# Shared weight places, ordered scores, squares summed on TensorE, and search state in PSUM, in a two-layer hybrid trunk

## The chip, the cores and the metric

The kernel runs on one core of one Trainium2 chip. The metric is device microseconds of one execution. The rows below come from one profiled execution of the kernel before.

## What is computed

The reference runs two residual layers over 1024 tokens of width 1024, and a final RMSNorm. Each layer is `h = h + mixer(rmsnorm(h))`, then `h = h + mlp(rmsnorm(h))`.

```python
# layer 0's mixer: sparse attention beside a pooling mixer
rel   = relu(einsum('bqhd,bsd->bqhs', qi, ki))
score = einsum('bqhs,bqh->bqs', rel, wi) * IDX_DIM ** -0.5     # causal
_, idx = lax.top_k(score, 256)                                 # per query
prob  = softmax(q @ k[idx] * Dh ** -0.5);  ya = prob @ v[idx]
yb    = (trailing means over 2/4/8/16 tokens - token) @ pool_w * pool_scale
out   = concat([ya, yb]) @ w_out
# layer 1's mixer: gated DeltaNet (short convolution, chunked delta rule)
# each MLP, hidden 4096
out   = square(relu(h @ w1)) @ w2
def rmsnorm(x, g): return x * rsqrt(mean(x * x, -1) + 1e-6) * g
```

## The kernel before

The tokens are kept transposed, in two halves of 512: `h[0]` and `h[1]`, each eight tiles of 128 features by 512 tokens. A full-precision product is three TensorE matmuls of 512 columns (`mm3`, L241 to L243) over values split in a high and a low part. Weights come in chunks of 256 KB: a DMA into a "raw" tile, a ScalarE copy that makes the high part (L167), and a GpSimd subtraction that makes the low part (L171). `prefetch` (L192) does this for a stream ("a", "m", or the layer 1 output weights "o"), into the rings that `room` gave the stream. A chunk takes two tiles of its ring, so ring "w" (4 tiles) has two places; the ring "wo" (2 tiles) has one, and stream "o" is loaded with `ahead=0`, which is when its chunk is wanted.

`norm_scale` squares the eight tiles on ScalarE (L301), adds them on VectorE (`add_square`, L304), sums the 128 partitions with four matmuls against a column of ones (`rstd_cols`, L284), takes the reciprocal root in twelve small VectorE operations (L260 to L265), and spreads the result over partitions with four transposes (L272).

`topk` (L607) finds each query's threshold bit by bit: 31 steps, each building a candidate (L655), counting scores against it (L629 on VectorE, L657 on ScalarE for some blocks), comparing the counts (L669) and keeping the candidate where it held (L670). Queries of blocks 2 and 3 are searched together in a stretch at 94 to 198 us, blocks 4 to 7 in another at 456 to 620 us. All small state of the search lies in SBUF. The steps run as a background job: the code that issues matmuls calls `tick`.

A scheduler orders each engine's instructions by the order in which the code names them and by priority. In the second stretch the first half's MLP is laid beside the search: `beside(us)` issues about that many microseconds of its matmuls between steps, with the amounts in `BESIDE` (L105): for index scores, for kept projections and the search, for the second attention, and for what remains of the background once the search is done. `next(att)` yields one step of attention. `odd_heads` does the same for layer 1, and takes the norm of `h[1]` before layer 1 at about 1654 us and of `h[0]` at about 947 us. `finish` (L1346) does the final norm of a half and writes it out.

PSUM has eight banks of 512 columns. In layer 0 they are 2 for "g", 1 for "o" and 5 for "t".

Of the kernel before, what the change touches and what calls it, by code (L numbers as in the profile page):

```python
# [35 lines left out]
BANKS = {"even": {"g": 2, "o": 1, "t": 5}, "odd": {"g": 2, "o": 1, "d": 2, "t": 3}}  # L36


C_ID, C_ONE = 0, P
C_ALL = P + 2  # L40
# [20 lines left out]
def const_tables():  # L61
# [4 lines left out]
    c[:, C_ONE:C_ONE + 2] = 1.0  # L66
# [38 lines left out]
BESIDE = (4.0, 3.4, 2.2, 6.0)  # L105


class Ring:


    def __init__(self, pool, name, n, cols, usual=None):
        self.pool, self.name, self.n, self.cols, self.usual = pool, name, n, cols, usual or cols
        self.count = 0
# [12 lines left out]
class Trunk:  # L126
    def __init__(self, ctx, tc, I, out):
# [8 lines left out]
        self.ident, self.ones = self.ca[:, C_ID:C_ID + P], self.ca[:, C_ONE:C_ONE + 2]  # L136
        wp = self.pool("weights")
        self.W, self.WM, self.raw = Ring(wp, "w", 4, 512), Ring(wp, "wm", 4, 512), Ring(wp, "raw", 4, 512)
# [40 lines left out]
    def plan(self, **streams):  # L179
# [3 lines left out]
        self.rings, self.ahead, self.loaded = {}, {}, dict.fromkeys(streams, 0)  # L183
# [95 lines left out]
    def rstd_cols(self, sq, n, out=None):  # L279

        nc = self.nc
        ps = self.bank()
        for c in range(4):
            nc.tensor.matmul(ps[:, 2 * c:2 * c + 2], sq[:, c * P:(c + 1) * P], self.ones[:, 0:2], start=True, stop=True)  # L284
# [5 lines left out]
    def norm_scale(self, h):  # L290
        return self.rstd(self.squares(h), D)
# [15 lines left out]
    def norm(self, h, gain, ring=None):  # L307

        return self.normed(h, gain, self.norm_scale(h), ring)
# [53 lines left out]
    def gained(self, h, k, x):  # L363

        nc = self.nc
        f, gain = self.T.get(), self.prm[:, R_MIX + k:R_MIX + k + 1]
# [6 lines left out]
    def even_scales(self, acc):  # L373

        r = self.rstd_cols(acc, D, self.small(4, "even_r"))
# [6 lines left out]
    def even_first(self):  # L382
# [9 lines left out]
        acc = self.T.get()  # L392
        for k in range(KT):
# [4 lines left out]
            if k + 1 < KT:  # L398
                load(k + 1)
            if k == KT - 2:  # L400
                nc.sync.dma_start(self.ca, self.I["ca"])
                nc.sync.dma_start(self.cx, self.I["ce"])
            self.gained(h, k, x)
            sq = self.T.get() if k else acc
            nc.scalar.activation(sq, h[k], AF.Square)
            if k:
                nc.vector.tensor_tensor(acc, acc, sq, op=OP.add)
# [8 lines left out]
        self.even_scales(acc)  # L416
# [4 lines left out]
    def even_second(self):  # L421
# [7 lines left out]
        self.even_scales(self.squares(hs))  # L429
# [177 lines left out]
    def topk(self, blocks, nv):  # L607
# [12 lines left out]
        cnt, sg, cur, cand, keep, t1, t2, most, top = (  # L620
# [821 lines left out]
```

## Time and profile before

| | us |
|---|---|
| median of 3 runs | 2864.97 |
| their range | 2862.25 to 2869.15 |
| the profiled execution | 2867.0 |
| its span, first to last instruction | 2865.2 |
| TensorE busy | 2678.5 (93%) |
| VectorE busy | 1711.5 (60%) |
| GpSimd busy | 1248.2 (44%) |
| ScalarE busy | 1187.8 (41%) |
| mean granted TensorE clock | 0.969 of 2.4 GHz |

A timeline line gives the start, the duration in us, the engine, the line of code, the operation, what is written from what is read, and in brackets the idle time before it with what ended it. A line of a view by line gives, after the bar, the time in us, the mean in ns of one, and the idle time before. In the view of stretches the columns of busy time are PE (TensorE), PEld (its weight loads), DVE (VectorE), ACT (ScalarE) and POOL (GpSimd), then the granted clock, the DMA share and GB/s.

### The profile page before, as it was taken

What the parts mean: (1) busy time and instruction counts of PE and PEld (TensorE: products, weight loads), DVE (VectorE), ACT (ScalarE), POOL (GpSimd) and SP (SyncE); (2) the same over time, 40 slices, a digit from 0 to 9 for tenths busy, and PEclk for the clock granted to TensorE, in tenths of its full rate; (3) what the DMA queues carried; (4) which work ended last, traced back from release to release, by engine and by line L of the source; (5) the groups of instructions that cost most, each with busy time, mean ns of one, the idle gap of its engine ahead of it and who ended that gap; (6) DMA issues with size and microseconds to landing.
All of it is one profiled execution on the core that took longest, in us unless ns stands there. A gap on an engine that the chain in (4) does not pass through costs nothing. (4 is left out here: it accounts for less than half of the span.)

```text
span 2865.2 us, 44751 instructions
## 1 busy us (share of the span) xinstructions
PE 2678.5 (93%) x16648; PEld 2105.1 (73%) x16648; DVE 1711.5 (60%) x3653; ACT 1187.8 (41%) x2475; POOL 1248.2 (44%) x1074
## 2 busy tenths in 40 slices
PE   8788997988999899999999999899999999899997
PEld 6556775766777677887777767677777777688886
DVE  6894469997524645564655677755655644733334
ACT  4545455763433443343432444433333323333332
POOL 6642536442234544444444444444443434544442
PEclk9889999998999899999999999999999999999999
DMA  5221222220112222222222211122222222333332
GB/s 166 60 73 41 92 67 85 84 90 30 49 61 80 75 80 79 74 71 78 74 81 72 75 52 53 56 71 70 75 75 74 64 67 85 100 109 97 96 96 77
DMA packets 119917, 218.82 MB, mean 76 GB/s; under 512 B 13970, under 2 KB 15122, under 8 KB 119698
## 3 DMA queue, kind: packets, MB, share of 16 engines
q1 hardware_dynamic: 119698, 215.95, 24.3%
q8 instruction: 131, 2.15, 0.3%
q14 instruction: 88, 0.72, 0.1%
HBM read 207.51 MB, written 4.19 MB: 74 GB/s over the span
## 5 line engine op out<-in xcount | busy, mean ns | idle before, releaser
L171 POOL TENSOR_TENSOR wm<-raw,wm 128x512 fp32r<-128x512 f32 x437 | 581.1, 1330 | 904.5 <-ACT wm L167 880.7
L167 ACT ACTIVATE wm<-raw 128x512 fp32r<-128x512 f32 x437 | 274.4, 628 | 690.7 <-PE ps_g L242 344.2
L171 POOL TENSOR_TENSOR w<-raw,w 128x512 fp32r<-128x512 f32 x196 | 259.1, 1322 | 310.2 <-ACT w L167 296.4
L827 DVE TENSOR_TENSOR h<-ps_d,h 128x512 f32<-128x512 f32 x392 | 266.6, 684 | 154.2 <-PE ps_d L243 152.2
L241 PE MATMUL ps_g<-x,w 128*128 128x512 f32 x648 | 265.0, 409 | 8.8 <-ACT w L167 7.2
L242 PE MATMUL ps_g<-x,w 128*128 128x512 f32 x648 | 263.7, 407 | 6.2 <-POOL x L171 4.0
L813 DVE SCALAR_TENSOR_TENSOR ps_g<-ps_g,temps 128x512 f32<-128x512 f32 x128 | 89.1, 696 | 300.7 <-ACT temps L811 300.7
L243 PE MATMUL ps_g<-x,w 128*128 128x512 f32 x648 | 263.3, 406 | 1.8 <-POOL w L171 1.8
L241 PE MATMUL ps_d<-y,wm 128*128 128x512 f32 x596 | 247.2, 415 | 7.6 <-DVE h L827 6.3
L242 PE MATMUL ps_d<-y,wm 128*128 128x512 f32 x596 | 238.9, 401 | 0.0
L243 PE MATMUL ps_d<-y,wm 128*128 128x512 f32 x596 | 238.5, 400 | 0.2 <-POOL wm L171 0.2
L167 ACT ACTIVATE w<-raw 128x512 fp32r<-128x512 f32 x196 | 122.9, 628 | 277.1 <-PE ps_g L242 208.4
L241 PE MATMUL ps_g<-xb,wm 128*128 128x512 f32 x512 | 204.7, 400 | 11.9 <-DVE y L171 7.6
L243 PE MATMUL ps_g<-xb,wm 128*128 128x512 f32 x512 | 204.4, 399 | 4.5 <-POOL wm L171 4.4
L242 PE MATMUL ps_g<-xb,wm 128*128 128x512 f32 x512 | 204.4, 399 | 0.6 <-POOL xb L171 0.6
L934 DVE SCALAR_TENSOR_TENSOR qkvz<-temps,conv,qkvz 128x512 f32<-128x512 f32 x144 | 137.3, 953 | 110.2 <-ACT qkvz L932 109.3
L241 PE MATMUL ps_g<-x,wm 128*128 128x512 f32 (+1 forms) x396 | 158.4, 400 | 6.1 <-ACT wm L167 4.7
L243 PE MATMUL ps_g<-x,wm 128*128 128x512 f32 (+1 forms) x396 | 157.7, 398 | 0.7 <-POOL wm L171 0.7
L242 PE MATMUL ps_g<-x,wm 128*128 128x512 f32 (+1 forms) x396 | 158.1, 399 | 0.0
L241 PEld LDWEIGHTS ps_g<-x,w 128*128 128x128 f32 x648 | 126.7, 196 | 41.1 <-ACT w L167 7.6
L242 PEld LDWEIGHTS ps_g<-x,w 128*128 128x128 f32 x648 | 126.0, 195 | 36.3 <-POOL x L171 5.3
L827 DVE TENSOR_TENSOR h<-ps_t,h 128x512 f32<-128x512 f32 x184 | 125.8, 686 | 42.4 <-PE ps_t L243 41.8
(446 smaller groups left out, 6134.9 us busy)
## 6 DMA issues: line engine op xcount, KB each, us to landing
raw<-in_w_dram SPq DMA_DIRECT2D x512, 256.0 KB, 2.6
raw<-in_woi_dram SPq DMA_DIRECT2D x128, 256.0 KB, 2.6
raw<-in_wei_dram SPq DMA_DIRECT2D x52, 256.0 KB, 2.7
raw<-in_weo_dram SPq DMA_DIRECT2D x32, 256.0 KB, 2.6
raw<-in_woo_dram SPq DMA_DIRECT2D x32, 256.0 KB, 2.7
h<-in_xt_dram SPq DMA_DIRECT2D x16, 256.0 KB, 3.7
out_dram<-temps SPq DMA_DIRECT2D x16, 256.0 KB, 2.1
at<-at SPq DMA_DIRECT2D x48, 64.0 KB, 2.0
```

Of the source, the lines that this page charges most:

```text
L167: self.nc.scalar.activation(out, in_, AF.Copy)
L171: eng.tensor_tensor(lo, full, hi.bitcast(F32), op=OP.subtract)
L241: mm(ps, wh, xh, start=start, stop=False)
L242: mm(ps, wh, xl, start=False, stop=False)
L243: mm(ps, wl, xh, start=False, stop=stop)
L813: nc.vector.scalar_tensor_tensor(ps, ps, 0.0, r, op0=OP.max, op1=OP.mult)
L827: nc.vector.tensor_tensor(h, ps, h, op=OP.add)
L934: nc.vector.scalar_tensor_tensor(acc, pin[:, j:j + 512], cw(j), acc, op0=OP.mult, op1=OP.add)
```

## The change

It has five parts.

1. Places. Ring "w" has two tiles instead of four. Layer 0 gets a second ring "w2" of two tiles, and layer 1 a ring "wo" of four tiles, shared by streams "a" and "o". `prefetch` takes the ring whose next place was loaded longest ago.
2. Sums of squares. `summed_squares` sums eight square tiles on TensorE into one PSUM accumulation: four matmuls of two columns for each tile, 32 a norm instead of four and seven VectorE additions. It is used for the first projection of each half, and for the norms that go through `norm`, which now include the one of `h[1]` before layer 1, and for `finish` of the second half. The ones come from a memset.
3. Search state. In `topk`, `cur`, `keep` and `top` lie in a PSUM bank "s" of their own; `cnt`, `cand`, `sg`, `most`, `t1` and `t2` stay in SBUF. Bank "t" has four instead of five.
4. Scale by gain. `gained` computes the low part with one VectorE operation instead of a VectorE multiplication and a subtraction on VectorE or GpSimd.
5. Order. The first eight steps of the second attention are each issued behind the last matmul so far, with 3.0 us of MLP after each. `BESIDE` changes.

```diff
-BANKS = {"even": {"g": 2, "o": 1, "t": 5}, ...}
+BANKS = {"even": {"g": 2, "o": 1, "s": 1, "t": 4}, ...}
-BESIDE = (4.0, 3.4, 2.2, 6.0)
+BESIDE = (4.0, 2.6, 2.8, 9.0, 3.0)
-        self.W, ... = Ring(wp, "w", 4, 512), ...
+        self.W, ... = Ring(wp, "w", 2, 512), ...
@@ prefetch
-            ring = rings[self.loaded[st] % len(rings)]
-            self.loaded[st] += 1
+            ring = min(rings, key=lambda r: r.loads[0])
+            self.loaded += 1
+            ring.loads.append(self.loaded)
+    def add_columns(self, ps, sq, start, stop):
+        for c in range(4):
+            self.nc.tensor.matmul(ps[:, 2 * c:2 * c + 2], sq[:, c * P:(c + 1) * P], self.ones[:, 0:2],
+                                  start=start and c == 0, stop=stop and c == 3)
+    def summed_squares(self, h):
+        ps = self.bank()
+        for k, t in enumerate(h):
+            sq = self.T.get()
+            self.nc.scalar.activation(sq, t, AF.Square)
+            self.add_columns(ps, sq, k == 0, k == KT - 1)
+        return ps
@@ norm
-        return self.normed(h, gain, self.norm_scale(h), ring)
+        return self.normed(h, gain, self.norm_scale(h, True), ring)
@@ gained
-        nc.vector.tensor_scalar(f, h[k], gain, None, op0=OP.mult)
...
-        self.rest(t[:, 512:1024], f, t[:, 0:512], k % 2 == 0)
+        nc.vector.scalar_tensor_tensor(t[:, 512:1024], h[k], gain, t[:, 0:512].bitcast(F32), op0=OP.mult, op1=OP.subtract)
@@ topk
-        cnt, sg, cur, cand, keep, t1, t2, most, top = (
-            small(n) for n in ("cnt", "sg", "cur", "cand", "keep", "t1", "t2", "most", "top"))
+        cnt, sg, cand, t1, t2, most = (small(n) for n in ("cnt", "sg", "cand", "t1", "t2", "most"))
+        state = self.bank("s")
+        cur, keep, top = (state[:, n * G:(n + 1) * G] for n in range(3))
@@ odd_heads
-                x[s] = self.normed(self.h[s], R_MIX + 8, self.norm_scale(self.h[s]))
+                x[s] = self.norm(self.h[s], R_MIX + 8)
@@ even layer, rings
-            self.room("a", self.W, self.WM, self.W, self.WM, self.W)
+            self.W2 = Ring(ep, "w2", 2, 512)
+            self.room("a", self.W, self.WM, self.W2)
@@ second attention
-                with self.tc.issue_after(self.last_matmul()):
-                    next(att)
+                for _ in range(8):
+                    with self.tc.issue_after(self.last_matmul()):
+                        next(att)
+                    beside(BESIDE[4])
@@ odd layer, rings
-            self.room("a", self.W, ahead=1)
-            self.room("o", Ring(op, "wo", 2, 512), ahead=0)
+            more = Ring(op, "wo", 4, 512)
+            self.room("a", self.W, more, ahead=1)
+            self.room("o", more, ahead=0)
@@ finish
-        r = self.norm_scale(self.h[s])
+        r = self.norm_scale(self.h[s], s == 1)
```

Three places show how instructions stand. The first is VectorE's row in a search of two blocks; `tk_cur`, `tk_keep` and `tk_top` are SBUF tiles, `ps_s` the new bank. Before:

```order
L655 TENSOR_SCALAR tk_cand<-tk_cur 128x2
L629 TENSOR_SCALAR junk,tk_cnt<-mask_76,tk_cand 128x384
L557 TENSOR_TENSOR temps<-ps_g,rb 128x512
L669 TENSOR_TENSOR tk_keep<-tk_cnt,tk_top 128x2
L559 COPY uhist<-temps 128x16
L670 COPY_PREDICATED tk_cur<-tk_keep,tk_cand 128x2
```

And after:

```order
L674 TENSOR_SCALAR tk_cand<-ps_s 128x2
L648 TENSOR_SCALAR junk,tk_cnt<-mask_78,tk_cand 128x384
L688 TENSOR_TENSOR ps_s<-tk_cnt,ps_s 128x2
L689 COPY_PREDICATED ps_s<-ps_s,tk_cand 128x2
L674 TENSOR_SCALAR tk_cand<-ps_s 128x2
L648 TENSOR_SCALAR junk,tk_cnt<-mask_78,tk_cand 128x384
```

The four operations of a step keep their order; L655, L669 and L670 have become L674, L688 and L689 with an operand in PSUM, and the counting operation has none.

The second place is TensorE at the norm of `h[1]` before layer 1; L284 and L289 are the column sums, L272 and L273 the transposes. Before:

```order
L241 MATMUL ps_d<-yh,wo 128x512
L284 MATMUL ps_t<-ca,temps 128x2 x4
L242 MATMUL ps_d<-yh,wo 128x512
L243 MATMUL ps_d<-yh,wo 128x512
L241 MATMUL ps_d<-y,wo 128x512
...
L241 MATMUL ps_d<-yh,wo 128x512
L242 MATMUL ps_d<-yh,wo 128x512
L272 MATMUL ps_t<-ca,rs_y 128x128 x4
```

And after:

```order
L242 MATMUL ps_d<-y,wm 128x512
L243 MATMUL ps_d<-y,wm 128x512
L244 MATMUL ps_d<-y,wm 128x512
L289 MATMUL ps_t<-ones,temps 128x2 x32
L273 MATMUL ps_t<-ca,rs_y 128x128 x4
L1074 MATMUL ps_t<-xxc,lm 32x32 x4
L1078 MATMUL ps_t<-dy,xtc 32x32 x4
```

Before, thirteen wide matmuls stand between the sums and the transposes; now the eight sets of sums stand together and nothing stands between them and the transposes.

The third place is the end of TensorE's row, at the final norm of the second half. Before:

```order
L242 MATMUL ps_t<-y,wm 128x512
L243 MATMUL ps_t<-y,wm 128x512
L284 MATMUL ps_t<-ca,temps 128x2 x4
L272 MATMUL ps_t<-ca,rs_y 128x128 x4
L1438 UNCONDITIONAL_BRANCH
```

And after:

```order
L243 MATMUL ps_t<-y,wm 128x512
L244 MATMUL ps_t<-y,wm 128x512
L289 MATMUL ps_t<-ones,temps 128x2 x32
L273 MATMUL ps_t<-ca,rs_y 128x128 x4
L1463 UNCONDITIONAL_BRANCH
```

All eight sets stand behind the last wide matmul.

## Rows read from the trace of the kernel before

**Rows 1.** The page's first part: busy time of each engine.

```profile
PE 2678.5 (93%) x16648; PEld 2105.1 (73%) x16648; DVE 1711.5 (60%) x3653; ACT 1187.8 (41%) x2475; POOL 1248.2 (44%) x1074
```

**Rows 2.** Stretches: ends and length, busy us by engine, TensorE's clock, DMA.

```profile
94.00:198.00 104.00, 86.04 (x330) 63.35 (x331) 95.59 (x255) 58.37 (x127) 56.78 (x45) 0.84 0.23 70
198.00:262.00 64.00, 51.23 (x269) 39.42 (x268) 38.73 (x103) 29.79 (x65) 21.03 (x15) 0.87 0.16 52
...
456.00:620.00 164.00, 142.07 (x565) 107.86 (x564) 151.18 (x320) 118.38 (x213) 81.62 (x61) 0.95 0.29 88
620.00:670.00 50.00, 31.39 (x118) 23.84 (x117) 48.78 (x85) 11.75 (x21) 16.11 (x11) 0.81 0.19 59
```

**Rows 3.** What TensorE waits for, whole span: us, times, longest us.

```profile
PE ps_d L243 <- POOL wo L171: 21.6, 22, 3.1
...
PE ps_t L359 <- DVE mx L711: 7.4, 1, 7.4
```

**Rows 4.** VectorE by line, 60 to 262 us: busy us, mean ns, idle.

```profile
L655 DVE TENSOR_SCALAR tk_cand<-tk_cur 128x2 int32<-128x2 int32 x30 | 15.8, 525 | 0.6
L670 DVE COPY_PREDICATED tk_cur<-tk_keep,tk_cand 128x2 f32<-128x2 uint32 x31 | 12.5, 404 | 0.7
L669 DVE TENSOR_TENSOR tk_keep<-tk_cnt,tk_top 128x2 f32<-128x2 f32 x31 | 11.2, 362 | 3.3 <-ACT junk L657 3.2
...
L304 DVE TENSOR_TENSOR temps<-temps 128x512 f32<-128x512 f32 x7 | 7.9, 1131 | 0.0
```

**Rows 5.** The same by line, 456 to 620 us.

```profile
L669 DVE TENSOR_TENSOR tk_keep<-tk_cnt,tk_top 128x4 f32<-128x4 f32 x31 | 12.3, 397 | 8.2 <-ACT junk L657 8.1
...
L655 DVE TENSOR_SCALAR tk_cand<-tk_cur 128x4 int32<-128x4 int32 x30 | 6.1, 203 | 0.7
L670 DVE COPY_PREDICATED tk_cur<-tk_keep,tk_cand 128x4 f32<-128x4 uint32 x31 | 5.9, 191 | 0.9
```

**Rows 6.** Timeline, VectorE in the first search: start, us, line, operation.

```profile
161.41 1.27 DVE L655 TENSOR_SCALAR tk_cand<-tk_cur 128x2 int32<-128x2 int32 x1
162.60 0.15 DVE L286 TENSOR_SCALAR rs_m<-ps_t 128x4 f32<-128x4 f32 x1
```

**Rows 7.** Timeline, GpSimd in the same stretch.

```profile
161.37 1.29 POOL L347 TENSOR_TENSOR q<-temps,q 64x512 fp32r<-64x512 f32 x1 [2.83 <-ACT q L167]
```

**Rows 8.** Durations of VectorE's line 655: ns shortest/median/longest.

```profile
L655 DVE TENSOR_SCALAR tk_cand<-tk_cur x62: 154/169/1281, 0.9 to 616.6; 128x2 int32<-128x2 int32 x31, 128x4 int32<-128x4 int32 x31
```

**Rows 9.** Durations of VectorE's line 286, which reads PSUM.

```profile
L286 DVE TENSOR_SCALAR rs_m<-ps_t x12: 147/162/163, 25.4 to 2852.2; 128x4 f32<-128x4 f32 x12
```

**Rows 10.** Durations of VectorE's line 260, which reads SBUF alone.

```profile
L260 DVE TENSOR_SCALAR rs_t<-rs_m x12: 162/169/386, 25.6 to 2852.4; 128x4 int32<-128x4 int32 x12
```

**Rows 11.** Timeline, TensorE: a norm's column sums at full clock.

```profile
24.40 0.95 PE L284 MATMUL ps_t<-ca,temps 128*128 128x2 f32 x8
```

**Rows 12.** Timeline, TensorE: such sums after a wait, at 915 us.

```profile
915.17 1.87 PE L284 MATMUL ps_t<-ca,temps 128*128 128x2 f32 x8 [3.55 <-DVE temps L304]
```

**Rows 13.** Timeline, TensorE: a wait for a shared output weight.

```profile
1332.94 0.50 PE L243 MATMUL ps_d<-yh,wo 128*128 128x512 f32 x1 [2.15 <-POOL wo L171]
```

**Rows 14.** Timeline, TensorE: the norm before layer 1, first half.

```profile
950.93 1.08 PE L284 MATMUL ps_t<-ca,temps 128*128 128x2 f32 x8 [1.30 <-DVE temps L304]
```

**Rows 15.** Timeline, TensorE: the norm before layer 1, second half.

```profile
1658.02 0.95 PE L284 MATMUL ps_t<-ca,temps 128*128 128x2 f32 x8
...
1663.92 0.62 PE L272 MATMUL ps_t<-ca,rs_y 128*128 128x128 f32 x4 [0.73 <-DVE rs_t L263]
```

**Rows 16.** Timeline, all engines: the end.

```profile
2847.84 0.40 PE L242 MATMUL ps_t<-y,wm 128*128 128x512 f32 x1
...
2848.08 0.39 PE L243 MATMUL ps_t<-y,wm 128*128 128x512 f32 x1
...
2851.13 1.05 PE L284 MATMUL ps_t<-ca,temps 128*128 128x2 f32 x8 [2.67 <-DVE temps L304]
...
2854.61 1.12 PE L272 MATMUL ps_t<-ca,rs_y 128*128 128x128 f32 x4 [2.43 <-DVE rs_y L265]
```

More of the change, by code (lines that the diff above doesn't have):

```diff
@@ L35 @@
 FILL = (5.6, 4.7)
-BANKS = {"even": {"g": 2, "o": 1, "t": 5}, "odd": {"g": 2, "o": 1, "d": 2, "t": 3}}
-C_ID, C_ONE = 0, P
-C_ALL = P + 2
+BANKS = {"even": {"g": 2, "o": 1, "s": 1, "t": 4}, "odd": {"g": 2, "o": 1, "d": 2, "t": 3}}
+C_ID, C_ALL = 0, P
 C_SWAP, C_CAUS = 0, P
@@ L182, in plan @@
         self.ready = {n: deque() for n in streams}
-        self.rings, self.ahead, self.loaded = {}, {}, dict.fromkeys(streams, 0)
+        self.rings, self.ahead, self.loaded = {}, {}, 0
         for n in streams:
@@ L279, in rstd_cols, with rstd_of @@
     def rstd_cols(self, sq, n, out=None):
+        ps = self.bank()
+        self.add_columns(ps, sq, True, True)
+        return self.rstd_of(ps, n, out)
+    def add_columns(self, ps, sq, start, stop):
[3 more added lines that the diff above has]
+    def summed_squares(self, h):
+        ps = self.bank()
+        for k, t in enumerate(h):
[3 more added lines that the diff above has]
+        return ps
+    def rstd_of(self, ps, n, out=None):
         nc = self.nc
-        ps = self.bank()
-        for c in range(4):
-            nc.tensor.matmul(ps[:, 2 * c:2 * c + 2], sq[:, c * P:(c + 1) * P], self.ones[:, 0:2], start=True, stop=True)
         m = self.small(4, "rs_m")
@@ L288, in rstd_cols, with norm_scale @@
         return self.rsqrt(m, 4, out)
-    def norm_scale(self, h):
+    def norm_scale(self, h, sums=False):
+        if sums:
+            return self.over_partitions(self.rstd_of(self.summed_squares(h), D))
         return self.rstd(self.squares(h), D)
@@ L363, in gained, with even_scales @@
     def gained(self, h, k, x):
[L365 to L367 removed]
+        nc, gain = self.nc, self.prm[:, R_MIX + k:R_MIX + k + 1]
         t = self.X.parts()
         nc.scalar.activation(t[:, 0:512], h[k], AF.Copy, scale=gain)
[L370 removed]
+        nc.vector.scalar_tensor_tensor(t[:, 512:1024], h[k], gain, t[:, 0:512].bitcast(F32), op0=OP.mult, op1=OP.subtract)
         x.append(t)
[L373 to L375 removed]
+    def even_scales(self, ps):
+        r = self.rstd_of(ps, D, self.small(4, "even_r"))
         n8 = self.small(4, "even_n8")
@@ L391, in even_first @@
         pss = [self.bank("g") for _ in keys]
-        acc = self.T.get()
+        sums = self.bank()
         for k in range(KT):
@@ L399, in even_first @@
                 load(k + 1)
+            if k == 3:
+                nc.sync.dma_start(self.ca, self.I["ca"])
             if k == KT - 2:
-                nc.sync.dma_start(self.ca, self.I["ca"])
                 nc.sync.dma_start(self.cx, self.I["ce"])
             self.gained(h, k, x)
-            sq = self.T.get() if k else acc
+            sq = self.T.get()
             nc.scalar.activation(sq, h[k], AF.Square)
-            if k:
-                nc.vector.tensor_tensor(acc, acc, sq, op=OP.add)
+            self.add_columns(sums, sq, k == 0, k == KT - 1)
             for n in range(2):
@@ L415, in even_first @@
                 self.chunk((key, n))
-        self.even_scales(acc)
+        self.even_scales(sums)
         pss.append(self.project(EVEN_A[2], x, tag="t"))
@@ L428, in even_second @@
             hs += [t[:, 0], t[:, 1]]
-        self.even_scales(self.squares(hs))
+        self.even_scales(self.summed_squares(hs))
         return hs
```

16 lines of the change are left out of this document (9 added, 7 removed).

## The prediction

> **What bounds the kernel now.** I read the busy times first, then a table of stretches, then what TensorE waits for, and last single lines. TensorE is busy 2678.5 of 2865.2 us [rows 1], so 187 us of idle time are all that any change of order can win, beside what a higher clock gives. The stretches show where the idle time lies [rows 2]: 18 us in 94 to 198 us and 13 in 198 to 262, 22 in 456 to 620, 19 in 620 to 670. In those four TensorE's granted clock is also lowest, 0.84, 0.87, 0.95 and 0.81. In the first and the third VectorE is the busier engine: 95.59 of 104 us and 151.18 of 164. There the threshold search runs. Over the whole span the largest sum of TensorE's waits is 21.6 us for the low part of a layer 1 output weight, 22 times, the longest single one is 7.4 us, the attention's for the row maxima [rows 3].
>
> **The search state in PSUM.** A bit step holds three tiny operations: candidate (L655), comparison (L669), keep (L670). In the first search they take 15.8, 11.2 and 12.5 us for 92 instructions, a mean of 525, 362 and 404 ns [rows 4], while the fastest candidate took 154 ns and half took 169 ns or less [rows 8]. The long executions are stalls. The candidate at 161.41 took 1.27 us beside a GpSimd subtraction that ran from 161.37 for 1.29 us, so both ended together [rows 6, 7]. The operation that followed it on VectorE, L286, reads PSUM and took 0.15 us [rows 6]; of its twelve executions none took over 163 ns [rows 9], whereas L260, the same size from SBUF alone, reached 386 [rows 10]. All three step operations get an operand in PSUM, so I take them at 150 ns: 92 x 0.15 = 13.8 us instead of 39.5, which frees 25.7 us of VectorE. The seven square additions of the second half, 7.9 us [rows 4], leave VectorE as well. Together VectorE loses 33.6 us where it was the bound.
>
> TensorE cannot follow the whole way: eight sets of column sums come to it there instead of one, 7 x 0.95 = 6.7 us [rows 11], and it has 86 us of its own in the 104, at a clock of 0.84. At full clock that work is some 86 x 0.84 = 72 us, about what VectorE then needs (95.6 - 25.7 = 69.9). Where two engines come out level, part of the gain is lost to their waits for each other; I take two thirds of the 33.6. **First search: -22 us**, bounds +7 (nothing gained, sums paid) and -34.
>
> In the second search the same lines take 12.3, 6.1 and 5.9 us for 92 instructions [rows 5], so 24.3 - 13.8 = 10.5 us go. This search is paced by MLP work laid beside it, of which the order has 48 matmuls fewer, so a shorter search is possible, but VectorE also does the adds of that MLP. **Second search: -6 us**, bounds 0 and -10.5.
>
> The Trainium skill states, in Perfetto Trace Analysis, section Optimizing Scalar/DVE Operations, that a DVE access costs about 60 ns of overhead on SBUF and about 125 on PSUM. By that rule 184 small operations would cost 184 x 65 ns = 12 us more, an estimate against the change; the trace disagrees, for L286 from PSUM has a median of 162 ns and L260 from SBUF one of 169 [rows 9, 10].
>
> **Gain scaling.** One VectorE operation replaces one or two. It reads two SBUF operands, so it may itself stall like the adds of L304 (1131 ns mean, [rows 4]). Eight times 1.1 us against the multiplication and half a subtraction is no change: 0, bounds -3 and +3, beside TensorE that waits for DMA in that stretch anyway.
>
> **Second attention's start.** TensorE waits 7.4 us for the row maxima [rows 3] in a stretch with 18.6 us idle and VectorE at 48.78 of 50 [rows 2]. The changed order has 24 and 12 wide matmuls between the first scores and the next, where there were 6 and 12: 18 x 0.24 = 4 us of cover (2848.08 - 2847.84 from one wide matmul to the next, [rows 16]), and more steps that follow at once. Some of the waited-for VectorE work remains. **-6 us**, bounds 0 and -10.
>
> **Shared places.** A typical wait is 2.15 us at 1332.94, for an output weight whose place came free late [rows 13]. Going through both orders, 23 of 32 output chunks had under 1.5 us of TensorE work between the last use of their place and their own first use; with the change 17 have, the middle ones of each group queueing behind their predecessor as before. So 6 of 23 parts of 21.6 us go, 5.6 us; three chunks of stream "a" and about five in layer 0 newly come that close, some 0.5 us each. **-2 us**, bounds +4 and -18.
>
> **Column sums.** One set (four matmuls, eight records) took 0.95 us at full clock [rows 11]. Seven sets more cost 6.7 us if exposed.
> - First projection, first half: between matmuls that wait for weights; +1.5 us, bounds 0 and 7.
> - Norm of `h[0]` before layer 1: one set behind a 1.30 us wait for the adds [rows 14], which goes: 6.7 - 1.3 = **+5 us**, bounds 1 and 8.
> - Norm of `h[1]` before layer 1: the set at 1658.02 and the transposes at 1663.92, with 0.73 us idle, had matmuls between [rows 15]. Now 32 sums, the root and the transposes stand in a row: 6.7 for the sums, some 2.4 for the root (the same twelve operations took that at the end [rows 16]), and 0.62 for the transposes [rows 15]: **+10 us**, bounds 2 and 14.
> - Final norm: from 2848.08 + 0.24 the eight sets need 7.6 us; the old way needed until 2851.13 + 1.05 = 2852.18. 2848.4 + 7.6 = 2856.0: **+4 us**, bounds 0 and 11. The squares are no limit, since the five square tiles in flight let the first sums start during the last matmuls' drain.
>
> **Four banks "t" instead of five** in layer 0: one evacuation less in flight, **+2.5 us**, bounds 0 and 8. The trace shows no wait that names a bank.
>
> The sum is -22 - 6 + 0 - 6 - 2 + 1.5 + 5 + 10 + 4 + 2.5 = -13 us. From the profiled execution's 2867.0 (2865.2 of span and 1.8 outside) this gives 2854; the median of the runs shown, 2865, is 2 lower, and from it the forecast is **2852 us**. The rivals are worked out from the median too.
>
> **Rivals.**
>
> *Sums at half clock: slower.* After a 3.55 us idle stretch the same eight records took 1.87 us instead of 0.95 [rows 11, 12]: as at the lower of the clock's two levels, 1.2 instead of 2.4 GHz. Sums give TensorE little to do and stand in a row at three places, 24 sets. At 0.92 us more each that is +22 us: -13 + 22 = +9, **2874 us**. It decides from 0.95 + 13 / 24 = 1.49 us a set. For it: the norm sums of before that came after a wait were long. Against it: the set at 2851.13 took 1.05 us even after 2.67 us of idling [rows 16], and the one at 950.93 1.08 [rows 14].
>
> *The stalls stay.* `cand` and `cnt` remain in SBUF, so the step operations still read or write it. If that is what GpSimd collides with, the first search gives only the additions, two thirds of 7.9: -22 becomes -5 and the second search 0: -13 + 17 + 6 = +10, **2875 us**. Against it: L286 writes SBUF from PSUM and never stalled [rows 9].
>
> *More than expected.* All waits for output weights go (-16 on top of -2), the first search falls by the 31 us of idle time in its two stretches and the attention's start by 9: -13 - 16 - 9 - 3 = -41, **2824 us**. For it: the places are loaded by age and the idle time is there to be won [rows 2, 3]. Against it: the middle chunks queue as before.
>
> *The gains are eaten.* The first search is held by TensorE's own 86 us and a low clock, so it gives 10 us instead of 22: -13 + 12 = -1, **2864 us**.
>
> **How the numbers follow.** Chances: the forecast 0.47, half clock 0.15, stalls stay 0.07, more than expected 0.18, gains eaten 0.13. The range reaches from the case of more to the half clock and the stalls: **2824 to 2876 us**; it leaves out half of the best case and the worse half of the two cases above the median, some 2 in 10. The likeliest case's own range is 2840 to 2862. What a measurement of this kernel can tell from no change is about 0.2%, 5.7 us. Faster by more: 0.47 x 0.92 + 0.18 + 0.13 x 0.15 = 0.63. Slower: 0.15 + 0.07, less 0.03 for their mild ends, and 0.01 of the last case: 0.20. Within: what remains, 0.17.
>
> **What would show it.** In the profile after, the three step operations should have means of 140 to 200 ns in both searches, and 94 to 262 us should be some 22 us shorter. The candidate at over 300 ns would prove the stalls wrong. The wide matmuls after each of the three blocks of sums should stand 0.24 us apart, and a set should take 0.95 us; 1.5 or more is the first rival. The last set should end some 8 us behind the last wide matmul. Waits for output weights should add up to 16 to 20 us; under 5 is the third rival. The forecast is wrong altogether if TensorE's idle time in the first search stays at 31 us.

## The result and the profile after

The changed kernel took 2908.07 us (median of 4 runs, 2898.70 to 2919.01) against 2863.61 us for the kernel before: a ratio of 1.0154, 95% interval 1.0115 to 1.0193. It is 44 us slower where 13 us less were forecast, and outside the range. The profiled execution has a span of 2907.9 us, 42.7 more than before.

The busy times after answer to [rows 1]:

```profile
PE 2736.7 (94%) x16928; PEld 2157.7 (74%) x16928; DVE 1654.1 (57%) x3610; ACT 1185.6 (41%) x2475; POOL 1230.5 (42%) x1067
```

TensorE idles less than before (171 us against 187), and the kernel is longer: the added time is TensorE's own. The stretches after, with the columns of [rows 2]:

```profile
94.00:198.00 104.00, 93.33 (x378) 71.41 (x378) 75.25 (x234) 57.11 (x124) 54.41 (x43) 0.85 0.23 72
198.00:262.00 64.00, 55.94 (x298) 42.86 (x298) 44.42 (x122) 35.11 (x78) 22.20 (x16) 0.92 0.18 58
456.00:620.00 164.00, 148.76 (x600) 116.20 (x598) 152.51 (x338) 122.28 (x220) 90.83 (x67) 0.94 0.31 93
620.00:670.00 50.00, 25.18 (x109) 19.87 (x110) 44.66 (x89) 9.64 (x19) 7.95 (x6) 0.73 0.12 38
```

Fixed stretches hide what moved, since the work is later. Both kernels issue the same 9392 wide matmuls (512 columns into 128 partitions), so I compare the times at which the n-th of them starts:

| stretch, by wide matmul | before, us | after, us | difference | forecast |
|---|---|---|---|---|
| start to 75 (first projection) | 33.6 | 41.0 | +7.4 | +1.5 |
| 75 to 600 (second half's sums, first search) | 212.9 | 204.7 | -8.2 | -22 |
| 600 to 2275 (second search and attention) | 548.3 | 545.8 | -2.5 | -9.5 |
| 2275 to 2775 (MLP) | 142.0 | 147.8 | +5.8 | 0 |
| 2775 to 3000 (norm of `h[0]`) | 67.9 | 80.3 | +12.4 | +5 |
| 3000 to 5225 and 5350 to 7700 (layer 1) | 1397.0 | 1406.6 | +9.6 | -2 |
| 5225 to 5350 (norm of `h[1]`) | 47.8 | 55.6 | +7.8 | +10 |
| 7700 to the last (MLP) | 398.6 | 404.2 | +5.6 | 0 |
| the end | 17.1 | 21.9 | +4.8 | +4 |

The search's step operations are what the prediction said. VectorE's lines between 60 and 250 us (busy us, mean ns) answer to [rows 4], and the durations of the candidate over the whole run (shortest, median, longest) to [rows 8]:

```profile
L689 DVE COPY_PREDICATED ps_s<-ps_s,tk_cand 128x2 f32<-128x2 uint32 x31 | 5.0, 162 | 0.5
L688 DVE TENSOR_TENSOR ps_s<-tk_cnt,ps_s 128x2 f32<-128x2 f32 x31 | 5.0, 161 | 7.4 <-ACT junk L676 7.2
...
L674 DVE TENSOR_SCALAR tk_cand<-ps_s 128x2 int32<-128x2 int32 x31 | 4.8, 155 | 0.5
```

```profile
L674 DVE TENSOR_SCALAR tk_cand<-ps_s x62: 142/159/164, 111.3 to 611.5; 128x2 int32<-128x2 int32 x31, 128x4 int32<-128x4 int32 x31
```

Means of 155 to 162 ns replace 362 to 525, and no candidate takes over 164 ns. The long executions are gone: 14.8 us for 93 operations, where 92 took 39.5.

What ate it is in TensorE's timeline. The sums of the second half's squares, x8 being the records of one set, answer to [rows 11]:

```profile
91.98 0.95 PE L289 MATMUL ps_t<-ones,temps 128*128 128x2 f32 x8
92.79 0.48 PE L242 MATMUL ps_g<-x,w 128*128 128x512 f32 x1
93.11 0.40 PE L243 MATMUL ps_g<-x,w 128*128 128x512 f32 x1
...
94.69 1.20 PE L289 MATMUL ps_t<-ones,temps 128*128 128x2 f32 x8
...
96.75 1.70 PE L289 MATMUL ps_t<-ones,temps 128*128 128x2 f32 x8
...
98.88 0.63 PE L243 MATMUL ps_g<-x,wm 128*128 128x512 f32 x1
```

The first set takes 0.95 us and a wide matmul behind it 0.40; from the third set on the sets take up to 1.70 and a wide matmul 0.63. The lower of the two clock levels (1.2 instead of 2.4 GHz) has come while the sums were running, and no wait preceded it. In the trace's records of the granted clock it lasts from 95.2 to 115.7 us, and the mean of this stretch is 0.60:

```profile
92.00:108.00 16.00, 16.00 (x74) 14.67 (x73) 3.89 (x19) 3.90 (x7) 2.71 (x3) 0.60 0.06 17
```

TensorE's records cover the whole of it, 16.00 of 16.00 us. The Trainium skill, TensorE: Matmul & The Clock Gate, section What's actually happening, has the clock go by how busy the array has been of late. Whether the trace agrees hangs on what counts as busy, which that section does not say: here the clock fell without a wait, while TensorE's records left no gap.

The same at the norm of `h[0]` before layer 1, where before there was one set [rows 14]:

```profile
949.86 6.58 PE L289 MATMUL ps_t<-ones,temps 128*128 128x2 f32 x40
...
956.87 0.63 PE L243 MATMUL ps_g<-xb,wm 128*128 128x512 f32 x1
...
963.27 1.70 PE L289 MATMUL ps_t<-ones,temps 128*128 128x2 f32 x8
...
967.96 0.63 PE L242 MATMUL ps_g<-xb,wm 128*128 128x512 f32 x1
```

Forty records (five sets) take 6.58 us, the later sets 1.70 each, and the matmuls are still at 0.63 us 18 us after the first set. At the norm of `h[1]` [rows 15] and at the end [rows 16], where no wide matmul stands between:

```profile
1673.39 0.39 PE L244 MATMUL ps_d<-y,wm 128*128 128x512 f32 x1
1673.62 8.73 PE L289 MATMUL ps_t<-ones,temps 128*128 128x2 f32 x64
1684.88 1.09 PE L273 MATMUL ps_t<-ca,rs_y 128*128 128x128 f32 x4 [2.53 <-DVE st L266]
...
1687.68 0.80 PE L242 MATMUL ps_g<-x,wo 128*128 128x512 f32 x1
```

```profile
2886.03 0.39 PE L244 MATMUL ps_t<-y,wm 128*128 128x512 f32 x1
...
2886.26 9.54 PE L289 MATMUL ps_t<-ones,temps 128*128 128x2 f32 x64
...
2898.23 1.11 PE L273 MATMUL ps_t<-ca,rs_y 128*128 128x128 f32 x4 [2.44 <-DVE rs_y L266]
```

Eight sets take 8.73 and 9.54 us, 1.1 to 1.2 us a set, instead of the forecast 7.6; at the second half's input and at the norm of `h[0]` eight come to 11.6 and 11.7. Behind the block at 1673.62 the root leaves TensorE idle for 2.53 us, and the matmul at 1687.68 runs at the lower level as well.

The waits after answer to [rows 3]:

```profile
PE ps_t L242 <- DVE mx L730: 20.4, 1, 20.4
PE ps_d L244 <- POOL wo L170: 17.6, 17, 3.7
PE ps_g L244 <- POOL wm L170: 13.8, 16, 2.0
```

### The profile page after: what moved, and what is told of

It is laid out like the page before. It is cut to its first block, busy times and chain, and to the rows that moved or that the text cites. A ratio compares the mean times of both kernels' runs of the same rounds, so it can differ in the third digit from the quotient of the medians.

```text
span 2907.9 us, 45254 instructions
## 1 busy us (share of the span) xinstructions
PE 2736.7 (94%) x16928; PEld 2157.7 (74%) x16928; DVE 1654.1 (57%) x3610; ACT 1185.6 (41%) x2475; POOL 1230.5 (42%) x1067
## 5 line engine op out<-in xcount | busy, mean ns | idle before, releaser
L170 POOL TENSOR_TENSOR wm<-raw,wm 128x512 fp32r<-128x512 f32 x427 | 566.3, 1328 | 872.8 <-ACT wm L166 825.3
L166 ACT ACTIVATE wm<-raw 128x512 fp32r<-128x512 f32 x427 | 267.8, 628 | 673.5 <-PE ps_g L243 317.3
L242 PE MATMUL ps_d<-y,wm 128*128 128x512 f32 x586 | 243.8, 416 | 5.7 <-DVE h L846 5.1
L244 PE MATMUL ps_d<-y,wm 128*128 128x512 f32 x586 | 235.8, 402 | 2.9 <-POOL wm L170 1.6
L243 PE MATMUL ps_d<-y,wm 128*128 128x512 f32 x586 | 235.8, 402 | 0.0
L170 POOL TENSOR_TENSOR w<-raw,w 128x512 fp32r<-128x512 f32 (+1 forms) x111 | 144.9, 1306 | 212.0 <-ACT w L166 178.4
L170 POOL TENSOR_TENSOR wo<-raw,wo 128x512 fp32r<-128x512 f32 x111 | 145.1, 1308 | 185.5 <-ACT wo L166 179.6
L242 PE MATMUL ps_g<-x,wm 128*128 128x512 f32 (+1 forms) x372 | 153.1, 411 | 5.0 <-ACT wm L166 3.6
L244 PE MATMUL ps_g<-x,wm 128*128 128x512 f32 (+1 forms) x372 | 151.6, 408 | 4.5 <-POOL wm L170 4.2
L243 PE MATMUL ps_g<-x,wm 128*128 128x512 f32 (+1 forms) x372 | 151.5, 407 | 3.4 <-DVE x L388 3.4
L166 ACT ACTIVATE wo<-raw 128x512 fp32r<-128x512 f32 x111 | 70.2, 633 | 188.5 <-PE ps_g L243 103.7
L170 POOL TENSOR_TENSOR wm above<-raw,wm above 128x512 fp32r<-128x512 f32 x72 | 93.4, 1298 | 104.8 <-ACT wm above L166 104.1
L242 PEld LDWEIGHTS ps_d<-y,wm 128*128 128x128 f32 x586 | 111.9, 191 | 34.4 <-DVE h L846 10.0
L166 ACT ACTIVATE w<-raw 128x512 fp32r<-128x512 f32 (+1 forms) x111 | 69.3, 624 | 159.2 <-PE ps_g L243 112.1
L244 PEld LDWEIGHTS ps_d<-y,wm 128*128 128x128 f32 x586 | 111.5, 190 | 27.7 <-POOL wm L170 2.4
```

The costliest lines, as they stand in the source:

```text
L166: self.nc.scalar.activation(out, in_, AF.Copy)
L170: eng.tensor_tensor(lo, full, hi.bitcast(F32), op=OP.subtract)
L242: mm(ps, wh, xh, start=start, stop=False)
L243: mm(ps, wh, xl, start=False, stop=False)
L244: mm(ps, wl, xh, start=False, stop=stop)
```

## The experiments

I call the loss through column sums **S**, through places **P**, through order **O**. Medians are in us; ratios are to the kernel before on the same chip, which took 2862.36 to 2864.71 us beside them. Small differences between two experiments are therefore taken each against its own kernel before, and are known to some 6 us; differences to the changed kernel, whose four runs lie 20 us apart, to some 12. The first four kernels start from the two ends: three are the changed kernel with one part undone, one is the kernel before with one part done.

**a1: the changed kernel without the column sums.**

```diff
-        return self.normed(h, gain, self.norm_scale(h, True), ring)
+        return self.normed(h, gain, self.norm_scale(h), ring)
... (the same for the two inputs and the final norm: additions on VectorE, one set)
```

> The changed kernel with the squares added on VectorE as before, one set of column sums for each norm; everything else as changed. Theory S (the column sums are the loss: TensorE at the lower clock during and after each block of eight sets): the stretches that grew at the five norms give back 7 us at the first projection, 6 at the second half's, 10 at the norm of h[0], 8 at the norm of h[1] and 5 at the end: 2908 - 36 = 2872 us. Rival P (the new places and the order of loads are the loss): at most 12 us back, 2896 us.

Measured 2857.11, ratio 0.9977 (0.9966 to 0.9987). The sums cost 51 us, and the other four parts together gain 5 us. By the stretches of the table a1 gives back 8.0, 11.9, 11.9, 4.5 and 5.8 us at the five sums, 42 in all, and 5.8 in the last MLP, which has no sums; c1 below shows what most of those 5.8 are. From matmul 75 to 600 it is 20 us ahead of the kernel before.

**a2: the changed kernel without the places.**

```diff
-        self.W = Ring(wp, "w", 2, 512)
+        self.W = Ring(wp, "w", 4, 512)
-            ring = min(rings, key=lambda r: r.loads[0])
+            ring = rings[self.loaded[st] % len(rings)]
... (and the rings "w2" and "wo" of both layers as before)
```

> The changed kernel with ring w of four tiles, wo of two for the output weights alone, and the choice of rings by turns, as before. Theory S: the two stretches of layer 1 that lost 5 and 4 us through late output weights give these back and no more, 2899 us. Rival P: most of the 43 us comes back, below 2880 us. A third way: nothing, since what waits for one place only waits elsewhere, 2908 us.

Measured 2884.09, ratio 1.0072 (1.0053 to 1.0090): 24 us back (known to some 12), between the theories.

**a3: the changed kernel with the old order of the second search and attention.**

```diff
-BESIDE = (4.0, 2.6, 2.8, 9.0, 3.0)
+BESIDE = (4.0, 3.4, 2.2, 6.0)
-                for _ in range(8):
-                    with self.tc.issue_after(self.last_matmul()):
-                        next(att)
-                    beside(BESIDE[4])
+                with self.tc.issue_after(self.last_matmul()):
+                    next(att)
```

> The changed kernel with the old amounts of MLP work beside the search and the old start of the second attention. The profile after shows one wait of 20.4 us for the row maxima at 635 us, where there were 7.4 and 5 shorter ones. Theory S: the new order only gathered the waits of that stretch into one, so 2908 us within 6. Rival O: the 20.4 us wait is a loss of the new order, 2908 - 15 = 2893 us.

Measured 2893.01, ratio 1.0105 (1.0090 to 1.0120): 15 us back, the rival's number but not its reason: a3 has the old order and waits as long.

```profile
PE ps_t L242 <- DVE mx L730: 20.3, 1, 20.3
```

Matmuls 600 to 2275 take as long as in the changed kernel (546.3 us); the profile of a3 is shorter by 5 us in each of the two stretches behind, 2275 to 2775 and 2775 to 3000, and by 8 in layer 1. Why is not shown.

**a4: the kernel before with only the search state in PSUM.**

```diff
-BANKS = {"even": {"g": 2, "o": 1, "t": 5}, ...}
+BANKS = {"even": {"g": 2, "o": 1, "s": 1, "t": 4}, ...}
+        state = self.bank("s")
+        cur, keep, top = (state[:, n * G:(n + 1) * G] for n in range(3))
... (and the ones from a memset, and an earlier load of the identity)
```

> The kernel before with only the search state moved to its PSUM bank (bank t has four), plus the ones column from a memset and the earlier load of the identity. The step operations take 150 to 170 ns as in the profile after. Theory V (VectorE bounds the first search): it ends some 15 to 25 us sooner and the second 5, so about 2845 us. Rival T (TensorE bounds it as soon as VectorE is relieved, and what follows waits anyway): -5 us, 2859 us, or no change at all.

Measured 2847.02, ratio 0.9950 (0.9933 to 0.9967): 15.3 us less. In the trace, wide matmuls 262 to 600 take 132.0 us instead of 145.7, 75 to 262 and 600 to 2275 gain 3 and 2 more. VectorE does not keep all that the step operations free: twelve additions of two SBUF operands (L329 before, L348 in a4) rise from 912 to 1285 ns on the mean, 4.5 us together.

The next four split S, and add one part to the state.

**b1 and b2: the changed kernel without the sums at the three norms (b1), or at the two inputs (b2).**

```diff
 b1
-                x[s] = self.norm(self.h[s], R_MIX + 8)
+                x[s] = self.normed(self.h[s], R_MIX + 8, self.norm_scale(self.h[s]))
... (the same for the norm of h[0] and the final one)
 b2
-        self.even_scales(self.summed_squares(hs))
+        ps2 = self.bank()
+        self.add_columns(ps2, self.squares(hs), True, True)
+        self.even_scales(ps2)
... (and additions on VectorE in the first half's loop)
```

> The changed kernel with the squares added on VectorE at the three norms (of h[0] and h[1] before layer 1, and the final one of the second half); the sums of the two inputs stay on TensorE. With all five gone the time was 2857.1 us. Theory S (every block of sums costs by itself, through its own length and the lower clock behind it): by the stretches of the profile 21 of the 51 us lie at the two inputs, so 2857 + 21 = 2878 us. Rival: the blocks cost little alone and the loss is one of their meeting with the places, below 2865 us.

> The other half: the squares of the two inputs added on VectorE, the three norms summed on TensorE. Theory S: 51 - 21 = 30 us stay, 2887 us, and the wide matmuls of the first projection reach the spacing of 0.23 us some 4 us sooner. Rival: 2900 us or more, the inputs' sums being covered by waits for weights as the prediction had them.

Measured 2884.22 (1.0048 to 1.0082) and 2880.20 (1.0033 to 1.0071): the norms' sums cost 24 us and the inputs' 28, 52 together against a1's 51. They add. The inputs, which the prediction had as nearly covered, cost about as much as the norms; the 28 hold some 5 us that are not the sums' own (c1).

**b3 and b4: state in PSUM with the gain scaling (b3), or with the new order (b4).**

```diff
 b3
+        nc.vector.scalar_tensor_tensor(t[:, 512:1024], h[k], gain, t[:, 0:512].bitcast(F32), op0=OP.mult, op1=OP.subtract)
 b4
+BESIDE = (4.0, 2.6, 2.8, 9.0, 3.0)     # and the new start of the attention
```

> The kernel before with the search state in PSUM and the gain scaled in one VectorE operation; sums, places and order as before. Against the state alone (2847.0 us): VectorE has eight multiplications less in the first search, so 5 us less, 2842 us, if VectorE still bounds it; 2847 us if not; over 2850 us if the operation with two SBUF operands stalls beside GpSimd as the additions did.

> The kernel before with the search state in PSUM and the new order of the second search and attention; sums, places and gain as before. Theory O (the new order starves TensorE once, in the 20 us wait for the row maxima): 2847 + 10 = 2857 us or more, with one wait of 15 to 20 us there. Rival (it only looked bad beside the other parts, and covers the attention's start as meant): 2847 - 6 = 2841 us.

Measured 2844.81 (0.9911 to 0.9945) and 2854.53 (0.9946 to 0.9975). Each against its own kernel before, they are 19.9 and 10.2 us faster, where a4 is 15.3: the gain scaling is worth 4.6 us and the order costs 5.1 by itself, both within the uncertainty. The order's wait for the row maxima is not 15 to 20 but 30.1 us; a4 has one of 20.7.

**c1: the changed kernel with one tile more taken, and nothing else.**

```diff
         sums = self.bank()
+        self.T.get()
         for k in range(KT):
```

> The changed kernel with one unused tile taken from the ring of temporaries ahead of the first x tile, so that this ring lies below ring x in SBUF again, as in the kernel before; nothing else. In the profile after, wide matmuls of the last 420 us stand 0.2305 us apart, where they stood 0.2278, and in every kernel with the inputs summed on TensorE ring x starts at an address equal to that of ring wm modulo 2048 bytes, in the others 320 bytes off. Theory A (the address sets the spacing): 0.2278 in that stretch again, 4 us less there, 2908 - 5 = 2903 us. Rival: the spacing hangs on something else of the input sums, 0.2305 stays.

Measured 2900.74, ratio 1.0117 (1.0092 to 1.0142), 7 us less; that difference alone is within the uncertainty, the spacing is not. TensorE's records in 2600 to 2800 us, first of the changed kernel and then of c1 (the second figure in brackets after the length is their number):

```profile
2600.00:2800.00 200.00, 200.00 (x870) 162.92 (x869) 69.81 (x108) 65.70 (x108) 93.94 (x73) 1.00 0.31 95
```

```profile
2600.00:2800.00 200.00, 200.00 (x880) 165.02 (x879) 72.09 (x112) 67.61 (x112) 94.77 (x74) 1.00 0.31 97
```

870 matmuls against 880 in the same 200 us of unbroken work at full clock. With the inputs summed on TensorE, ring x is first used ahead of the ring of temporaries and so gets another place in SBUF; that alone made each of these matmuls 2.7 ns longer. In the last MLP, 7700 to the last, it is 4.7 us (404.2 against 399.5). a1 and b2 also undo it, since they take the inputs' sums away.

**c2: state, gain scaling, and the new places in layer 1 alone.**

```diff
+            more = Ring(op, "wo", 4, 512)
+            self.room("a", self.W, more, ahead=1)
+            self.room("o", more, ahead=0)
... (layer 0's rings by turns)
```

> State in PSUM and gain scaling (2844.8 us) with the new places in layer 1 alone: ring w of two tiles, ring wo of four shared by both streams and picked by age; in layer 0 rings w and w2 stand by turns where the two places of w stood, and sums and order are as before. Theory L (sharing moves the wait from output weights to MLP and projection weights): 1000 to 1640 us gets 8 to 12 us longer, later stretches give some back, 2844.8 + 9 = 2854 us. Rival (the places cost only together with the sums, as the 24 us and the 5 us by difference suggest): 2845 us within 3.

Measured 2845.99 (0.9921 to 0.9954): no cost on balance. Against b3, matmuls 3000 to 5225 take 8.3 us longer and 5225 to 5350 5.3, but 7100 to 7700 8.7 less.

**c3: the changed kernel with more columns of ones.**

```diff
-        cp.tile([P, 2], F32, name="ones")
+        cp.tile([P, 96], F32, name="ones")
-            self.nc.tensor.matmul(ps[:, 2 * c:2 * c + 2], sq[:, c * P:(c + 1) * P], self.ones[:, 0:2], ...)
+            self.nc.tensor.matmul(ps[:, c * 96:(c + 1) * 96], sq[:, c * P:(c + 1) * P], self.ones, ...)
... (and one column in 96 read behind them)
```

> The changed kernel with a ones tile of 96 instead of 2 columns, so that each of the 188 sums matmuls writes 96 equal columns, of which one is read; the weight loads are the same. Theory C (the sums cost most through the lower clock, in their own length and in the wide matmuls behind them): sets take 0.95 to 1.1 us throughout, the wide matmuls behind stay 0.23 us apart, and 15 to 25 us of the 51 come back, 2888 us. Rival W (they cost through their number): 2908 us, or 2915 if wider sums take longer.

Measured 2873.37, ratio 1.0029 (1.0019 to 1.0039): 35 of the 51 us are back, more than C asked. The same number of sums, with 48 times the columns, is shorter (the scheduler also put the eight sets of the second half's input in one row). That input, in the timeline and in the view of stretches, where the granted clock is 1.00 instead of 0.60, and then the end:

```profile
86.46 7.28 PE L289 MATMUL ps_t<-ones,temps 128*128 128x96 f32 x64
```

```profile
86.00:102.00 16.00, 16.00 (x104) 14.33 (x103) 13.31 (x60) 9.27 (x20) 5.19 (x6) 1.00 0.09 29
```

```profile
2853.39 7.28 PE L289 MATMUL ps_t<-ones,temps 128*128 128x96 f32 x64
2863.11 0.65 PE L273 MATMUL ps_t<-ca,rs_y 128*128 128x128 f32 x4 [2.44 <-DVE rs_y L266]
```

Eight sets take 7.28 us instead of 9.54, 0.91 each, and the transposes behind the root run at 0.65 instead of 1.11 us. Of the 35 us the stretches put 4.8, 2.7, 14.6, 2.2 and 2.7 at the five sums, 27 where a1 gives back 42: about two thirds of what the sums cost there was the clock, if c3's change of arrangement is left aside. The other 8 lie in layer 1, where a1 gives back 2. At the second half's input the full clock brings only 3 us of a1's 12; TensorE then waits for weights there (2.35 us at 110.68).

**c4: state, gain scaling, and the second half's additions into PSUM.**

```diff
+    def squares_in_bank(self, h):
+        acc = self.bank()
+        for k, t in enumerate(h):
+            sq = self.T.get() if k else acc
+            self.nc.scalar.activation(sq, t, AF.Square)
+            if k:
+                self.nc.vector.tensor_tensor(acc if k < KT - 1 else sq, acc, sq, op=OP.add)
+        return sq
```

> State in PSUM and gain scaling (2844.8 us), with the seven additions of the second half's squares on VectorE as before, but into a PSUM bank, the last one into SBUF for the column sums. Those additions took 1.13 us on the mean before, 0.66 at best. Theory V: with one operand in PSUM they take 0.69 us, 3 us less of VectorE, and 1 to 3 us of time, 2843 us. Rival: they are covered, 2845 us.

Measured 2834.59, ratio 0.9895 (0.9879 to 0.9910): the best kernel of all, 10 us below b3 where 3 were expected. Its additions, answering to the last of [rows 4]:

```profile
L324 DVE TENSOR_TENSOR ps_t<-ps_t,temps 128x512 f32<-128x512 f32 x6 | 4.1, 688 | 0.0
```

688 ns instead of 1131 before and 1098 in b3. The profiled executions of b3 and c4 lie 14.0 us apart; 7.4 of that fall to matmuls 75 to 1300, where the additions stand and what follows, and the rest is spread.

Terms of the places, the order and the additions were still open after these twelve.

**d1: state, gain scaling and all new places. d2: state, gain scaling and the new start of the second attention with the old amounts.**

```diff
 d2
+BESIDE = (4.0, 3.4, 2.2, 6.0, 3.0)     # and the eight steps of the start
```

> State in PSUM and gain scaling (2844.8 us) with the new places in both layers, sums and order as before. Theory J (the places cost only in company: they leave shorter reserves of loaded weights, and the stretches that the sums slow use them up): 2847 us within 4. Rival (layer 0's places cost by themselves): 2855 us or more, with the loss between 456 and 620 us.

> State in PSUM and gain scaling (2844.8 us) with the new start of the second attention (eight steps, each behind the last matmul, 3.0 us of MLP work after each), and the old amounts of work beside the search. In the profiles the wait for the row maxima ends when VectorE has made the masks of all four blocks, 20.7 us with the old order and 30.1 with the new. Theory M (both orders leave that wait; the new amounts have spent the MLP work that could have stood beside the masks): 2845 us within 4 with the old amounts. Rival (the new start puts the attention's scores ahead of the MLP and so makes the wait longer): 2852 us or more.

Measured 2853.00 (0.9941 to 0.9974) and 2841.97 (0.9908 to 0.9938). The places cost 9 us without sums, in neither expected way: the trace has most of the loss in layer 1 (matmuls 2775 to 7700, +8 of 9 us). The new start gains 2 us, within the uncertainty; by difference the order's loss lies with the new amounts of work.

**d3: c4 with every row of eight additions in PSUM.**

```diff
-        return self.rstd(self.squares(h), D)
+        return self.rstd(self.squares_in_bank(h), D)
```

> State in PSUM and gain scaling, with the additions of squares into a PSUM bank for the second half's input (2834.6 us so far) and for every norm that adds eight squares in a row. Theory V (the additions stall only where GpSimd works beside them, and they are on the path before layer 1 and each MLP): 1 to 5 us less, 2831 us. Rival: the bank held during the additions is missing elsewhere, since layer 1 has three, 2838 us or more.

Measured 2844.04 (0.9919 to 0.9948), 9 us above c4, as the rival had it in size: matmuls 5225 to 5350, at the norm of `h[1]`, take 53.7 us instead of 44.9. That a bank is what is missing there is not shown; no wait of TensorE in that stretch names one.

**e1: c4 and d2's start together. e2: the changed kernel with c3's ones, c1's tile and d2's amounts.**

> State in PSUM, gain scaling, additions of the second half's squares into a PSUM bank, and the new start of the second attention with the old amounts beside the search. Gains that add: 2834.6 - 2.8 = 2832 us. Rival: the start's gain depends on where the search ends, and is gone, 2835 us or more.

> The changed kernel with three edits: 96 columns of ones in the sums, the ring of temporaries below ring x again, and the old amounts of work beside the search (the new start stays). If the costs add: 2873.4 - 5 (address) - 10 (amounts) = 2858 us. Rival (they stand for each other): 2870 us.

Measured 2837.51 (0.9893 to 0.9922) and 2861.59, ratio 0.9992 (0.9982 to 1.0001). The start's gain does not add to c4. Three small edits bring the changed kernel from 44 us slower to no measurable difference; matmuls of 2600 to 2800 us stand as close there as in c1 (880 records).

## Why the prediction was wrong

**The step that failed is the price of a set of sums.** "Seven sets more cost 6.7 us if exposed" took 0.95 us from a single set between wide matmuls, and held it for rows of eight. The rival "Sums at half clock" had the mechanism, with a chance of 0.15, and placed its decision at 1.49 us a set. The sets reached 1.70 inside a row, 1.1 to 1.5 on the mean of eight; a1 puts the price at 51 us, some 5 of them the place of ring x, and c3 gives 35 back with the lower clock largely gone from the rows of sums. That rival too was too small at 2874 us: its 1.49 us a set was not passed on the mean, but it counted 24 sets and left out the wide matmuls behind them (0.63 us where they took 0.40) and the two inputs. Its counterevidence, 1.05 us for the set at 2851.13 [rows 16], was a row after a wait and one set long, and so told nothing of a row of sets.

A row that warned of it was not read. "In those four TensorE's granted clock is also lowest" is wrong for the kernel before: its clock is 0.87 in 905 to 1000 us, where the norm of `h[0]` stands that was to get seven sets more.

```profile
905.00:1000.00 95.00, 78.68 (x311) 62.05 (x310) 61.62 (x100) 41.34 (x75) 46.89 (x40) 0.87 0.23 70
```

**First projection, +1.5 forecast, +7.4 measured.** "Between matmuls that wait for weights" was wrong. Behind its first matmul the kernel before waits only 2.7 us there, 0.5 of them for a weight, and the clock was still to rise. One of its rows shows full clock at 17 us:

```profile
16.98 0.39 PE L242 MATMUL ps_g<-x,w 128*72 128x512 f32 x1
```

TensorE after:

```profile
6.27 1.84 PE L289 MATMUL ps_t<-ones,temps 128*128 128x2 f32 x8 [6.27 <-ACT temps L424]
...
8.97 1.85 PE L289 MATMUL ps_t<-ones,temps 128*128 128x2 f32 x8
...
22.77 0.63 PE L243 MATMUL ps_g<-x,wm 128*72 128x512 f32 x1
...
24.95 0.39 PE L244 MATMUL ps_g<-x,wm 128*128 128x512 f32 x1
```

The sums alternate with wide matmuls of 0.63 us, and full clock comes after 23 us, 7 us later. The trace's records of the granted clock begin with that rise: at 16.58 us before, at 23.56 after, at 13.61 in c3, where the sums have 96 columns.

**The search state, -22 and -6 forecast.** The mechanism was right, and the mean durations too. By itself (a4) it gave 15.3 us instead of 28. The first search's part, 16.4 us from matmul 75 to 600, is about two thirds of the 25.7 that are there without the additions. With all parts but the sums (a1) that stretch is 20 us shorter, near the forecast 22; in the changed kernel the sums took 12 of them back. The second search gives 2 us (600 to 2275), for the waits behind it only move (next).

**Second attention, -6 forecast.** VectorE ends the second search by making masks for four blocks (L718), and then finds the row maxima (L730). After:

```profile
631.37 0.81 DVE L718 SCALAR_TENSOR_TENSOR mask<-junk,score 128x640 bf16<-128x640 bf16 x1
...
653.29 1.22 DVE L718 SCALAR_TENSOR_TENSOR mask<-junk,score 128x1024 bf16<-128x1024 bf16 x1
654.44 0.68 DVE L730 CUSTOM_DVE_ANT_0 probs<-ps_t,mask 128x512 f32<-128x512 f32 x1
```

Block 4's mask is ready at 632 us, but the first row maximum stands behind the masks of the other three, at 654, and TensorE waits 20.4 us (the waits above). The state alone has a like wait (20.7, a4), the new order 30.1 without the other parts (b4), the new start with old amounts 17.1 (d2). Before, the waits for VectorE stood apart:

```profile
PE ps_t L359 <- DVE h L827: 8.5, 4, 4.3
PE ps_t L359 <- DVE mx L711: 7.4, 1, 7.4
```

These (600 to 680 us) and 2.7 us more come to 18.6 us; after, it is 25.4, 20.4 of them in one piece. So the cover of "18 x 0.24 = 4 us" was counted against 7.4 us, the last of several waits for a VectorE that was busy 48.78 of 50 us [rows 2]. With the faster search TensorE stands before all four masks at once, which the prediction did not count, and the new order did not change that: with the old one the changed kernel waits 20.3 us (a3).

**Shared places, -2 forecast.** Counting distances in the order found which output chunks stop waiting: 17 wait, as counted, for 17.6 us (the waits above), inside the 16 to 20 that were to show it. It missed who waits instead. For the low part of weights in ring "wm" TensorE waited 5.1 us before, and 13.8 after:

```profile
PE ps_g L243 <- POOL wm L171: 5.1, 9, 1.1
```

TensorE's waits in layer 1's first half, first of b4 (old places) and then of a1 (new places):

```profile
PE ps_d L243 <- POOL wo L170: 6.3, 6, 2.2
...
PE ps_g L243 <- POOL wm L170: 0.7, 3, 0.3
```

```profile
PE ps_g L244 <- POOL wm L170: 7.3, 8, 1.4
PE ps_d L244 <- POOL wo L170: 4.7, 4, 2.7
```

For output weights it waits 1.6 us less, for MLP weights 6.6 more. Alone the places cost 2 to 9 us (c2, d1, known to some 6), with the sums 24 (a2, known to some 12). So the two seem to reinforce each other; by which path is not settled. That a short wait can cost more than its length shows one place in the trace after, in layer 1, though nothing shows that the places caused this wait:

```profile
2308.05 0.40 PE L243 MATMUL ps_d<-yh,wo 128*128 128x512 f32 x1
2310.30 0.36 PE L1078 MATMUL ps_t<-dy,xtc 32*32 32x32 f32 x5 [1.86 <-ACT dy L166]
...
2323.33 0.63 PE L244 MATMUL ps_d<-y,wm 128*128 128x512 f32 x1
...
2325.74 0.40 PE L244 MATMUL ps_d<-y,wm 128*128 128x512 f32 x1
```

Behind a wait of 1.86 us the granted clock is at its lower level for 13.7 us and the wide matmuls take 0.63 us, some 7 us lost for less than 2 waited.

**Gain scaling** (0, measured -4.6 within the uncertainty) was right. **The end** (+4, measured 4.8) was right in size, with sets longer than forecast (9.54 us instead of 7.6). **The norm of `h[1]`** (+10, measured +7.8) was too dear: by a1 the sums have 4.5 of it, and 3.3 stay without them. **Four banks** (+2.5) were not tried apart; they are in a4.

The parts measured by themselves, each against its own kernel before, give -15.3 (state), -4.6 (gain), +5.1 (order) and +8.7 (places), -6.1 in all; a1, which has these four, is at -5.3. What remains to +44.5 is the sums, the place of ring x that comes with them, and what they do to the rest.

## What to carry to other kernels

A row of narrow matmuls is not priced by one of them: ask what the clock does during the row and for the wide matmuls behind it, and take a stretch of the trace in which such a row has already run. Where VectorE's operations stalled beside GpSimd, one operand in PSUM ended it here, for tiny state (525 to 155 ns) and for 512-wide additions (1131 to 688) alike. Keeping the additions on VectorE with a PSUM accumulator was worth 10 us at the second half's input, where moving them to TensorE cost; doing it at every norm lost 9 of them (d3). And an experiment that gives the expected number may do so for another reason: a3 did, and only its trace tells.

## What was not expected of the hardware

- The place of a tile in SBUF set the pace of matmuls: 0.2305 us apart with ring x at the address of ring wm modulo 2048 bytes, 0.2278 with it 320 bytes off (c1, e2), about 4 us over the last 1600. Why is not shown.
- A caution in reading, not a fact of the chip: the view of stretches gives a granted clock of 1.00 for 12 to 25 us of the changed kernel, where wide matmuls run at 0.63 us:

```profile
12.00:25.00 13.00, 13.00 (x47) 9.89 (x47) 3.53 (x5) 6.14 (x11) 3.27 (x3) 1.00 0.53 191
```

The trace's records of the granted clock begin only at 23.56 us, and the view counts what lies ahead of them as full. At the start the durations tell the level, not that column.
